# A hybrid attention/SSD decoder layer on one core: last SSD root on VectorE, projection tokens split in pieces, loads further ahead, first quad without hops, conv weights stored later

## The chip, the core and the metric

The kernel runs on one core of one Trainium2 chip. The core has a matrix engine (TensorE, PE in the profile; PEld is its loading of the stationary operand), a vector engine (VectorE, DVE), a scalar engine (ScalarE, ACT), a general engine (GpSimd, POOL) and an engine that issues the DMAs here (SyncE, SP). Each works through its own instructions in order and waits on semaphores for the others. The metric is the device time of one execution in microseconds (us). Before the change three runs gave a median of 2215.1 us (2215.06 to 2215.61).

## The reference

One decoder layer with 2048 tokens and a width of 1024, in float32 (cut to what matters):

```python
h = modulate(rmsnorm(x, norm1_w), shift1, scale1)
proj = h @ w_in
q, k, v, z, xbc, dt_raw = jnp.split(proj, [o1, o2, o3, o4, o5], axis=-1)
q, k = rope(q, positions), rope(k, positions)
attn = sliding_window_attention(q, k, v, sinks)          # window 128
xbc = jax.nn.silu(causal_depthwise_conv(xbc, conv_w, conv_b))
xs, Bm, Cm = jnp.split(xbc, [SSM_WIDTH, SSM_WIDTH + SSM_GROUPS * D_STATE], axis=-1)
y = ssd_chunked_scan(xs, dt, A, Bm, Cm, d_skip) * jax.nn.silu(z)
yg = y.reshape(b, s, SSM_GROUPS, SSM_WIDTH // SSM_GROUPS)
yg = yg * lax.rsqrt(jnp.mean(yg * yg, axis=-1, keepdims=True) + EPS)
x = x + gate1 * (jnp.concatenate([attn, yg * ssm_norm_w], axis=-1) @ w_out)
h = modulate(rmsnorm(x, norm2_w), shift2, scale2)
x = x + gate2 * ((jax.nn.silu(g) * u) @ w_down)          # g, u = split(h @ w_gate_up)
return rmsnorm(x, final_norm_w)
```

The scale, shift and gate vectors come from `silu(c) @ w_ada + b_ada`.

## The kernel before

**Tiling.** The tokens are taken in four blocks (b = 0 to 3) of 512, each of four tiles (t) of 128. Every large product is made of three matmuls: each operand is split into a high part (a copy in a shorter format, made by ACT) and a low part (the remainder, made by DVE), and `mm3` adds high·high, high·low and low·high. A weight is split by `weight`: L274 on ACT and L275 on DVE. Where a weight serves several blocks the split pair is stored to memory (L278) and loaded again by later blocks as one pair (L270, 512 KB) in place of the raw weight (L273, 256 KB).

**Stages.** In the order in which PE runs them: an opening, then for each block the projections `queries`, `keys_values`, `convolved` (the causal convolution, eight channels c, weights `w_x`) and `gated` (z). Between them stand `out_proj(0)` (443 to 509 us), `out_proj(1)` (582 to 635 us) and, from 703.5 us, 22 quads, which compute the gate and up projection of the first half of the tokens. Later come the second half and the down projection.

**Hops.** Attention (`attentions`) and the scan (`ssds`) of a block consist of small steps with few matmuls each. They are woven into the large stages: generators whose steps (`hops`) are taken by `tick(ratio)` after each piece of a large stage, `ratio` being the number of hops for each piece. A pending entry `[n, root]` runs after n ticks. Through the projections PE's order is the order of the program text; the orders of DVE, ACT, POOL and SP are laid by the compiler's scheduler from program order and dependencies, except that `behind(engine)` ties an instruction behind the last one written for that engine.

**What the change touches.** `ssds` ends each tile with a group norm: L813 to L815 form the mean square, `rsqrt` (L246) its root (13 small operations on POOL, L252 to L257, behind L249 and L250 on DVE), `normed` (L734) scales by it on ACT, and the four transposes L739 follow on PE. `mixed` (L827) loads the finished attention and scan outputs of a block (the mix, eight channels) and splits them, L832 on ACT and L833 on DVE; out_proj reads channels 0 to 3 with the first half of a weight and 4 to 7 with the second. `out_proj` loads x (L842), adds the gated product (L849), stores `mid`, and sums the squares (L292); its `root` (L297, four matmuls against ones) gives the reciprocal norm, which `spread` (L333) puts on all partitions. `operands_first`, `operands_between` and `sums_ahead` (L953) make the operands of the quads during out_proj(1), conv(3) and gated(3), and `operands_kept` (L973) splits the last ones within the first quad (L907 on ACT, L908 on DVE or POOL). In the attention, L651 are the score matmuls, L660 their masking on DVE, L669, L670, L673 to L676 and L679 the softmax, L685, L687, L694 and L696 the product with the values. L204 (DVE) belongs to the modulation vectors, L492 and L493 end a channel of the convolution, L510 to L517 are its taps.

Of the kernel before, what the change touches and what calls it, by code (L numbers as in the profile page):

```python
# [32 lines left out]
TMP, M1, M2, M4 = 8, 3, 8, 4  # L33
MIX, MIX2, MIX1, RATIO_UP = 0.78, 1.1, 1.25, 0.7
HALF = 32
# [9 lines left out]
def hymba_layer(ctx, tc, xT, xtok, pos, wada, wadk, vecs, rows, wq, wkv, wz, wx, wo, wgu, wd, outT):  # L45
# [442 lines left out]
    def convolved(b, h):  # L488
# [7 lines left out]
        for c in range(8):  # L496
            ps = dense()
            for half in range(2):
                if half:
                    if ending:  # L500
                        end(*ending.pop())
                    yield
                whi, wlo = weight(wx[c, half], T, ("x", c, half), b == 0)
                for i in range(4):
                    k = 4 * half + i
                    ws = slice(i * P, (i + 1) * P)
                    mm3(ps, whi[:, ws], wlo[:, ws], h[k][0], h[k][1], k == 0, k == KT - 1)
# [190 lines left out]
    def ssds(b, stepping, m):  # L698
# [46 lines left out]
        for t in range(NT):  # L745
# [70 lines left out]
            rs = small([P, 2], "rs", 2)  # L816
            rsqrt(rs, ss, 2, nc.gpsimd, "rss", sb)
            out = (y, o, ts, rs)
# [7 lines left out]

    def mixed(b, mix, cs, into):  # L827
        for c in cs:
            hi, lo = into(c)
            m = lo.bitcast(F32)  # L830
            nc.sync.dma_start(m, spill[b][c])
            nc.scalar.activation(hi, m, AF.Copy)  # L832
            nc.vector.tensor_tensor(lo, m, hi.bitcast(F32), ALU.subtract)  # L833
            mix.append((hi, lo))

    def out_proj(b, y_of, mix, bank_of, acc, norm=None, each=lambda c: None):
        for c in range(KT):
            ps = bank_of(c)
            for half in range(2):
                if half:  # L840
                    x = tmp()
                    nc.sync.dma_start(x, xT[b, c])  # L842
                    yield
                whi, wlo = weight(wo[c, half], T, ("o", c, half), b == 0, b > 1)
                for i in range(4):
                    k = 4 * half + i
                    ws = slice(i * P, (i + 1) * P)
                    mm3(ps, whi[:, ws], wlo[:, ws], mix[k][0], mix[k][1], k == 0, k == KT - 1)
            nc.vector.scalar_tensor_tensor(x, ps, gate1[:, c:c + 1], x, ALU.mult, ALU.add)  # L849
            nc.sync.dma_start(mid[b][c], x)  # L850
            square_into(acc, x, c == 0, nc.vector if b < 2 else nc.gpsimd)
            each(c)
            yield

        def root():
            y_of[b] = rstd(acc, st=norm and norm())
        if norm is None:
            pending.append([2 if b else 9, root])
        else:
            for _ in range(2):  # L860
                yield
            root()
        yield
# [89 lines left out]
    def sums_ahead(s, bc):  # L953

        for k in range(4):
            h = fetched_mid(s, k, ((1, 1),))
            for at, src in (((0, 1), scaled_01[k]), ((0, 0), scaled_d[s][0][k]), ((1, 0), scaled_d[s][1][k])):
                h[at] = fetched_scaled(src)
            yield
            with behind(mybir.EngineType.DVE):  # L960
# [3 lines left out]
            nc.vector.scalar_tensor_tensor(t2, h[0, 0], shift_of(k, 0), t3, ALU.add, ALU.add)  # L964
            nc.vector.scalar_tensor_tensor(t4, h[1, 0], shift_of(k, 1), t2, ALU.add, ALU.subtract)
            if k < 3:
                for to, x in zip(raw_d[k], (h[1, 1], t3, t2, t4)):
                    nc.sync.dma_start(to, x)
            else:
                sums_ahead.last = dict(zip(("b22", "t3", "t2", "t4"), (h[1, 1], t3, t2, t4)))  # L970
            yield

    def operands_kept(ops):  # L973
        for n, src in zip(("t2", "t3", "b22", "t4"), (2, 1, 0, 3)):
# [5 lines left out]
            for k, x in enumerate((*got, sums_ahead.last[n])):  # L980
                if n == "b22":
                    shifted(ops[n][k], x, shift_of(k, 1))
                else:
                    kept(ops[n][k], x, nc.vector if n == "t2" else nc.gpsimd)

# [479 lines left out]
    def beside(main, ratio):  # L1465
        for i, _ in enumerate(main):
            yield i
            tick(ratio)

# [36 lines left out]
    with tc.manual_schedule(engines={mybir.EngineType.PE}):  # L1506
# [35 lines left out]
        for _ in range(4):  # L1542
            tick(MIX2)
        mixed(0, mix, range(KT), lambda c: operand())
        run(g, MIX1)
        run(out_proj(0, y_of, mix, lambda c: dense(), sums()), MIX1)
# [9 lines left out]
        bp = early.enter_context(tc.tile_pool(name="b0", bufs=1, reuse_waits="tile"))  # L1556
        mixed(1, mix, range(KT), lambda c: pair("b", 12, pool=bp))
        ops = {}
        operand_tiles(ops, bp, ("b11",), 12)
        for i in range(6):  # L1560
            take(conv, 1)
            tick(0.5)
            if i == 2:
                dg = diagonal(y_of[0])
            if i == 4:
                bcs = [spread(y_of[0], bc=side_bank(2), dg=dg)]
        prepared(3)
        firsts = operands_first(0, ops, bcs, (0,))
# [6 lines left out]
        for i in beside(chain(conv, gated(3, h)), 0.5):  # L1575
            if i == 3:
                dg = diagonal(y_of[1])
            if i == 5:
                drain(firsts)
                bcs.append(spread(y_of[1], bc=side_bank(3), dg=dg))  # L1580
                firsts = operands_between(0, ops, bcs)
            if i == 10:
                drain(firsts)
                firsts = sums_ahead(0, bcs)
            next(firsts, None)
# [15 lines left out]
    operands_kept(ops)  # L1601
    for _ in beside(main, RATIO_UP):
        if not sides:
            break
# [9 lines left out]
    def loaded(b, c):  # L1614
        mixed(b, mixes[b], (c,), lambda c: pair("mo", 11, pool=op))

# [149 lines left out]
```

## Time and profile before

| | before |
|---|---|
| median of three runs | 2215.1 us |
| profiled execution, its own time | 2213.34 us |
| its span in the trace | 2211.6 us |
| mean granted TensorE clock | 0.989 |
| idle time of PE in the span | 56.1 us |

The profile is of one execution. A timeline row gives start, length, engine, line, operation, output and inputs by the names of the program, shapes, and in brackets the idle time of the engine ahead of it with what ended that time. Times of one row can overlap the next by some hundredths, since the operations of an engine are pipelined. A window row gives the busy time of each engine in a stretch, with the count of instructions, the granted clock of PE (1.00 is full), the share of the DMA engines in use and what they moved.

### The profile page before, as it was taken

The page shows a single profiled execution, that of the slowest core. Times are in us where ns is not written, and L with a number is a line of the kernel's source. Part 1 is how long each engine was busy: PE and PEld are TensorE (multiplying, and loading weights), DVE is VectorE, ACT ScalarE, POOL GpSimd, SP SyncE. Part 2 cuts the span into 40 slices and gives each one's busy share as a digit, 9 for nine tenths or more (in the row PEclk, how much of TensorE's full clock was granted, in tenths as well). Part 3 has the DMA queues.
Part 4 walks back from the last instruction along what each step waited for, and adds up shares of the span by engine and source line. Part 5 has one row for each costly group of instructions (what it writes and reads, how often), then busy time and mean ns, then how long its engine had stood idle before and what let it go on. Part 6 is the DMA issues. An engine that isn't in the chain of part 4 may idle for free.

```text
span 2211.6 us, 33250 instructions
## 1 busy us (share of the span) xinstructions
PE 2155.5 (97%) x10984; PEld 1776.0 (80%) x10984; DVE 1656.8 (75%) x3139; ACT 1010.6 (46%) x2121; POOL 568.3 (26%) x714
## 2 busy tenths in 40 slices
PE   8989998999999999999999999999999999999998
PEld 6879897878778677788888888788888888788887
DVE  6987756776668767688887768878888775786575
ACT  3674634653545555433335445533333334554441
POOL 0213343323102311144442221233322321210011
PEclk9999999999999999999999999999999999999999
DMA  7998888697999422333344687735555536678553
GB/s 271 325 363 303 285 245 278 216 354 231 352 321 330 163 90 86 118 111 112 98 134 154 213 265 263 270 126 177 177 173 186 162 121 218 238 263 275 182 164 103
DMA packets 289756, 470.96 MB, mean 213 GB/s; under 512 B 27440, under 2 KB 97072, under 8 KB 289584
## 3 DMA queue, kind: packets, MB, share of 16 engines
q1 hardware_dynamic: 289008, 468.32, 63.4%
q8 instruction: 86, 1.41, 0.3%
q14 instruction: 86, 0.70, 0.1%
q10 hardware_dynamic: 576, 0.52, 0.1%
HBM read 333.93 MB, written 134.81 MB: 212 GB/s over the span
## 4 chain that ended last, share of the span: by engine, by line
PE 51%; DMA 2%; DVE 2%; POOL 1%; ACT 0%; issue 0%; SPq 0%; DVEq 0%; ACTq 0%; POOLq 0%
PE d L1144 15%; PE d L1014 6%; PE d L1012 6%; PE d L1013 6%; PE d L1285 1%; PE am L1014 1%; PE am L1012 1%; PE am L1013 1%; PE sm L1014 1%; PE sm L1012 1%; PE sm L1013 1%; DMA a<-act_t 1%; PE d L282 1%; PE d L283 1%; PE d L284 1%
## 5 line engine op out<-in xcount | busy, mean ns | idle before, releaser
L1144 PE MATMUL d<-a,w 128*128 128x512 f32 x1716 | 403.6, 396 | 3.6 <-DVE w L1140 2.0
L1144 PEld LDWEIGHTS d<-a,w 128*128 128x128 f32 x1716 | 321.9, 188 | 82.8 <-DVE w L1140 2.9
L1013 PE MATMUL d<-b,w 128*128 128x512 f32 x924 | 366.4, 397 | 0.8 <-POOL b L908 0.8
L1012 PE MATMUL d<-b,w 128*128 128x512 f32 x924 | 365.9, 400 | 0.9 <-ACT t L1044 0.9
L1014 PE MATMUL d<-b,w 128*128 128x512 f32 x924 | 366.0, 398 | 0.0
L873 ACT ACTIVATE w<-s 128x512 fp32r<-128x512 f32 x176 | 110.9, 632 | 219.6 <-PE d L1014 171.9
L1013 PEld LDWEIGHTS d<-b,w 128*128 128x128 f32 x924 | 174.6, 189 | 41.0 <-POOL b L908 1.7
L1012 PEld LDWEIGHTS d<-b,w 128*128 128x128 f32 x924 | 174.2, 189 | 41.1 <-ACT t L1044 1.3
L1014 PEld LDWEIGHTS d<-b,w 128*128 128x128 f32 x924 | 173.8, 188 | 40.0 <-issue 0.4
L282 PE MATMUL d<-w,hl 128*128 128x256 f32 (+1 forms) x592 | 175.2, 296 | 4.2 <-DVE s L515 4.2
L283 PE MATMUL d<-w,hl 128*128 128x256 f32 (+1 forms) x592 | 169.7, 287 | 0.1
L284 PE MATMUL d<-w,hl 128*128 128x256 f32 (+1 forms) x592 | 169.5, 286 | 0.0
L874 DVE TENSOR_TENSOR w<-s,w 128x512 fp32r<-128x512 f32 x176 | 157.8, 898 | 4.3 <-ACT w L873 3.8
L1126 DVE TENSOR_TENSOR a<-a 128x512 fp32r<-128x512 f32 x154 | 108.8, 721 | 50.7 <-ACT a L1125 50.3
L1140 DVE TENSOR_TENSOR w<-raw,w 128x512 fp32r<-128x512 f32 x156 | 111.9, 726 | 38.6 <-ACT w L1139 38.5
L1125 ACT ACTIVATE a<-a 128x512 fp32r<-128x512 f32 x154 | 95.9, 628 | 93.2 <-DMA a<-act_t 57.0
L873 ACT ACTIVATE w<-raw 128x512 fp32r<-128x512 f32 x132 | 83.1, 631 | 118.8 <-PE d L1014 46.2
L292 POOL TENSOR_TENSOR acc<-acc,t 128x512 f32<-128x512 f32 x35 | 52.2, 1492 | 331.4 <-ACT t L291 320.5
L282 PE MATMUL d<-hl,w 128*128 128x512 f32 x320 | 133.7, 418 | 0.7 <-DMA w<-w_x 0.7
L1139 ACT ACTIVATE w<-raw 128x512 fp32r<-128x512 f32 x156 | 90.7, 587 | 81.0 <-PE d L1144 52.3
L284 PE MATMUL d<-hl,w 128*128 128x512 f32 x320 | 127.3, 398 | 0.0
L283 PE MATMUL d<-hl,w 128*128 128x512 f32 x320 | 126.9, 397 | 0.0
(418 smaller groups left out, 4798.5 us busy)
## 6 DMA issues: line engine op xcount, KB each, us to landing
raw<-in_wgu_dram SPq DMA_DIRECT2D x176, 256.0 KB, 2.8
w<-w_x SPq DMA_DIRECT2D x48, 512.0 KB, 6.0
act_t<-t SPq DMA_DIRECT2D x88, 256.0 KB, 3.2
a<-act_t SPq DMA_DIRECT2D x88, 256.0 KB, 4.3
act_b<-t SPq DMA_DIRECT2D x66, 256.0 KB, 2.0
a<-act_b SPq DMA_DIRECT2D x66, 256.0 KB, 4.1
aw<-in_wada_dram SPq DMA_DIRECT2D x64, 256.0 KB, 4.8
raw<-wd_s SPq DMA_DIRECT2D x64, 256.0 KB, 3.0
```

The costliest lines, as they stand in the source:

```text
L282: nc.tensor.matmul(out, ahi, bhi, start=first, stop=False)
L283: nc.tensor.matmul(out, ahi, blo, start=False, stop=False)
L284: mm3.last = nc.tensor.matmul(out, alo, bhi, start=False, stop=last)
L873: nc.scalar.activation(hi, x, AF.Copy)
L874: eng.tensor_tensor(lo, x, hi.bitcast(F32), ALU.subtract)
L1012: nc.tensor.matmul(out, ahi, bhi, start=first and k == 0, stop=False, skip_group_check=True)
L1013: nc.tensor.matmul(out, ahi, blo, start=False, stop=False, skip_group_check=True)
L1014: mm3.last = nc.tensor.matmul(out, alo, bhi, start=False, stop=k == 3, skip_group_check=True)
L1125: nc.scalar.activation(hi, raw, AF.Copy)
L1126: nc.vector.tensor_tensor(lo, raw, hi.bitcast(F32), ALU.subtract)
L1140: nc.vector.tensor_tensor(w[1], raw, w[0].bitcast(F32), ALU.subtract)
L1144: mm3.last = nc.tensor.matmul(ps, w[x][:, ws], act[k][y], start=new and k == 0 and x + y == 0, stop=k == KP - 1 and x == 1, skip_group_che ...
```

## The change

The diff does the following.

1. The split pairs of the convolution's weights are stored when block 1 uses them, not block 0. So conv(1) loads the raw weights and splits them once more, and conv(2) is the first to load the pairs.
2. In `ssds` the root of the last tile of each block runs on DVE (nine operations, L260 to L262) in place of POOL.
3. `mixed` issues its eight loads at once and returns a generator that splits two channels at a time, each tied behind the last instruction written for ACT and for DVE. One pair is split after each piece of gated(2), or of conv(3) ahead of out_proj(1); what is left is split ahead of out_proj. The old form stays in `loaded`, for blocks 2 and 3.
4. `out_proj` loads the x of the next channel one channel ahead (through `load_x`, L345). The root of out_proj(1) runs one tick later, the spreads move by a piece, and `sums_ahead` starts a piece earlier and keeps two loads in flight.
5. In `operands_kept` the remainders of t3 are made by DVE; only those of t4 stay on POOL. The first six pieces of the quads tick with ratio 0, the others with 0.75 (0.7 before).

```diff
@@ constants @@
-MIX, MIX2, MIX1, RATIO_UP = 0.78, 1.1, 1.25, 0.7
+MIX, MIX2, MIX1, RATIO_UP = 0.78, 1.1, 1.25, 0.75
@@ convolved @@
-                whi, wlo = weight(wx[c, half], T, ("x", c, half), b == 0)
+                whi, wlo = weight(wx[c, half], T, ("x", c, half), b == 1)
@@ ssds @@
-            rsqrt(rs, ss, 2, nc.gpsimd, "rss", sb)
+            rsqrt(rs, ss, 2, nc.vector if t == NT - 1 else nc.gpsimd, "rss", sb)
@@ mixed @@
+        got = []
         for c in cs:
             hi, lo = into(c)
-            m = lo.bitcast(F32)
-            nc.sync.dma_start(m, spill[b][c])
-            nc.scalar.activation(hi, m, AF.Copy)
-            nc.vector.tensor_tensor(lo, m, hi.bitcast(F32), ALU.subtract)
-            mix.append((hi, lo))
+            nc.sync.dma_start(lo.bitcast(F32), spill[b][c])
+            got.append((hi, lo))
+
+        def split():
+            for n, (hi, lo) in enumerate(got):
+                with behind(mybir.EngineType.Activation):
+                    nc.scalar.activation(hi, lo.bitcast(F32), AF.Copy)
+                with behind(mybir.EngineType.DVE):
+                    nc.vector.tensor_tensor(lo, lo.bitcast(F32), hi.bitcast(F32), ALU.subtract)
+                mix.append((hi, lo))
+                if n % 2:
+                    yield
+        return split()
@@ out_proj @@
+        nxt = load_x(b, 0)
         for c in range(KT):
-            ps = bank_of(c)
+            ps, x = bank_of(c), nxt
             for half in range(2):
                 if half:
-                    x = tmp()
-                    nc.sync.dma_start(x, xT[b, c])
+                    nxt = load_x(b, c + 1) if c < KT - 1 else None
                     yield
...
-            pending.append([2 if b else 9, root])
+            pending.append([3 if b else 9, root])
@@ sums_ahead @@
+        held = [load(0)]
+        yield
+        held.append(load(1))
+        yield
+        for k in range(4):
+            got = summed(k, held.pop(0))
...
+            yield
+            if k < 2:
+                held.append(load(k + 2))
+                yield
@@ operands_kept @@
-                    kept(ops[n][k], x, nc.vector if n == "t2" else nc.gpsimd)
+                    kept(ops[n][k], x, nc.gpsimd if n == "t4" else nc.vector)
@@ main program @@
-        mixed(0, mix, range(KT), lambda c: operand())
-        run(g, MIX1)
+        split = mixed(0, mix, range(KT), lambda c: operand())
+        for _ in beside(g, MIX1):
+            next(split, None)
+        drain(split)
...
-        mixed(1, mix, range(KT), lambda c: pair("b", 12, pool=bp))
+        split = mixed(1, mix, range(KT), lambda c: pair("b", 12, pool=bp))
...
         for i in range(6):
             take(conv, 1)
             tick(0.5)
-            if i == 2:
+            if i > 1:
+                next(split, None)
+            if i == 1:
                 dg = diagonal(y_of[0])
-            if i == 4:
+            if i == 3:
                 bcs = [spread(y_of[0], bc=side_bank(2), dg=dg)]
+        drain(split)
...
-            if i == 3:
+            if i == 4:
                 dg = diagonal(y_of[1])
...
-            if i == 10:
-                drain(firsts)
-                firsts = sums_ahead(0, bcs)
+            if i == 9:
+                last_of, firsts = firsts, sums_ahead(0, bcs)
+                drain(last_of)
...
-    for _ in beside(main, RATIO_UP):
+    for _ in beside(main, lambda i: RATIO_UP if i >= 6 else 0):
```

In the changed kernel the lines of `mixed` are L837 (ACT, was L832) and L839 (DVE, was L833). Three places show how the orders move.

DVE near the end of gated(2), where a scan step ends (L808, L809), before:

```order
L660 ISA ast 128x1
L833 TENSOR_TENSOR hl_5311<-hl_5311 128x512
L833 TENSOR_TENSOR hl_5315<-hl_5315 128x512
L808 TENSOR_TENSOR m_5019<-m_5019,sm 128x512
L669 TENSOR_SCALAR ast<-ast 128x4
L809 SCALAR_TENSOR_TENSOR m_5019<-m_5019,m_4726 128x512
L670 TENSOR_TENSOR ast<-row,ast 128x4
L833 TENSOR_TENSOR hl_5319<-hl_5319 128x512
```

DVE at the same scan step in the changed kernel (its first two splits are hl_5335 and hl_5337):

```order
L660 ISA ast 128x1
L808 TENSOR_TENSOR m_5063<-m_5063,sm 128x512
L669 TENSOR_SCALAR ast<-ast 128x4
L809 SCALAR_TENSOR_TENSOR m_5063<-m_5063,m_4770 128x512
L670 TENSOR_TENSOR ast<-row,ast 128x4
L754 TENSOR_TENSOR m_5324<-st,dtv 128x512
L755 TENSOR_TENSOR m_5325<-st,row 128x512
L761 TENSOR_TENSOR m_5333<-sm,upper 128x256
L839 TENSOR_TENSOR hl_5335<-hl_5335 128x512
L839 TENSOR_TENSOR hl_5337<-hl_5337 128x512
```

And DVE some 45 rows later in the changed kernel, around the start of out_proj(0), with the splits of channels 4 to 7:

```order
L787 TENSOR_TENSOR m_5659<-st,ex 128x512
L275 TENSOR_TENSOR w<-raw,w 128x512
L728 TENSOR_TENSOR m_5652<-m_5652,m_5333 128x512
L839 TENSOR_TENSOR hl_5343<-hl_5343 128x512
L839 TENSOR_TENSOR hl_5345<-hl_5345 128x512
L527 SCALAR_TENSOR_TENSOR so<-s,d 128x256
L839 TENSOR_TENSOR hl_5347<-hl_5347 128x512
L839 TENSOR_TENSOR hl_5349<-hl_5349 128x512
```

All eight splits move from ahead of L808 to behind it, the last four of them up to the start of out_proj(0).

DVE around the start of out_proj(1) (b is the tile of a split mix channel), before: the last row of one group of maskings, then the last five splits.

```order
L660 ISA ast 128x1
L833 TENSOR_TENSOR b<-b 128x512 x3
L493 SCALAR_TENSOR_TENSOR sx<-s 128x512
L833 TENSOR_TENSOR b<-b 128x512
L669 TENSOR_SCALAR ast<-ast 128x4
L833 TENSOR_TENSOR b<-b 128x512
L204 ISA aw,part<-aw,csil,vec 128x512
```

The same place in the changed kernel, from the last masking of the next group on, with channels 4 and 5 and then 6 and 7:

```order
L839 TENSOR_TENSOR b<-b 128x512 x2
L675 TENSOR_TENSOR ast<-ast 128x4
L493 SCALAR_TENSOR_TENSOR sx<-s 128x512
L669 TENSOR_SCALAR ast<-ast 128x4
L676 RECIPROCAL ast<-ast 128x4
L204 ISA aw,part<-aw,csil,vec 128x512
L204 ISA part 128x1
L670 TENSOR_TENSOR ast<-row,ast 128x4
L204 ISA aw,mod<-aw,csil,part 128x512
L204 ISA mod 128x1
L1468 TENSOR_TENSOR dsh<-mod 128x4
L839 TENSOR_TENSOR b<-b 128x512 x2
```

The last four splits move behind one more group of four maskings (L660) and the last two behind L675 and what follows it.

ACT at the end of the third tile of ssds(1) (t = 2), during queries(3), at 514 us, before:

```order
L734 ACTIVATE m_6059<-m_6059,rs 128x256 x2
L687 COPY m_6406<-am 128x4x128
L687 COPY m_6406<-at 128x4x128
L673 ACTIVATE m_6340,ast<-m_6340,ast 128x256 x2
L673 ACTIVATE m_6343,ast<-m_6343,ast 128x256 x2
L742 ACTIVATE m_6219<-st,vec 128x128 x4
```

The same in the changed kernel:

```order
L687 COPY m_6450<-am 128x4x128
L673 ACTIVATE m_6384,ast<-m_6384,ast 128x256 x2
L673 ACTIVATE m_6387,ast<-m_6387,ast 128x256 x2
L687 COPY m_6450<-at 128x4x128
L674 ACTIVATE ast<-ast 128x4
L734 ACTIVATE m_6105<-m_6105,rs 128x256 x2
L679 ACTIVATE m_6384<-m_6384,ast 128x256 x2
L679 ACTIVATE m_6387<-m_6387,ast 128x256 x2
L742 ACTIVATE m_6265<-st,vec 128x128 x4
```

L734 moves from ahead of an attention step's L687 and L673 to behind them.

More of the change, by code (lines that the diff above doesn't have):

```diff
@@ L953, in sums_ahead, with load @@
     def sums_ahead(s, bc):
-        for k in range(4):
+        def load(k):
             h = fetched_mid(s, k, ((1, 1),))
@@ L958, in sums_ahead, with summed @@
                 h[at] = fetched_scaled(src)
-            yield
+            return h
+        def summed(k, h):
             with behind(mybir.EngineType.DVE):
@@ L965, in sums_ahead @@
             nc.vector.scalar_tensor_tensor(t4, h[1, 0], shift_of(k, 1), t2, ALU.add, ALU.subtract)
+            return h[1, 1], t3, t2, t4
+        held = [load(0)]
[4 more added lines that the diff above has]
+            got = summed(k, held.pop(0))
             if k < 3:
-                for to, x in zip(raw_d[k], (h[1, 1], t3, t2, t4)):
+                for to, x in zip(raw_d[k], got):
                     nc.sync.dma_start(to, x)
             else:
-                sums_ahead.last = dict(zip(("b22", "t3", "t2", "t4"), (h[1, 1], t3, t2, t4)))
+                sums_ahead.last = dict(zip(("b22", "t3", "t2", "t4"), got))
             yield
+            if k < 2:
+                held.append(load(k + 2))
+                yield
     def operands_kept(ops):
@@ L1467, in beside @@
             yield i
-            tick(ratio)
+            tick(ratio(i) if callable(ratio) else ratio)
     def run(main, ratio):
@@ L1614, in loaded @@
     def loaded(b, c):
-        mixed(b, mixes[b], (c,), lambda c: pair("mo", 11, pool=op))
+        hi, lo = pair("mo", 11, pool=op)
+        m = lo.bitcast(F32)
+        nc.sync.dma_start(m, spill[b][c])
+        nc.scalar.activation(hi, m, AF.Copy)
+        nc.vector.tensor_tensor(lo, m, hi.bitcast(F32), ALU.subtract)
+        mixes[b].append((hi, lo))
     def first_output():
```

## The prediction

> **What bounds the kernel now.** I read the shares of busy time first, then the PE rows that begin after idle time, then windows laid around those rows.
>
> ```profile
> span 2211.6 us, 33250 instructions
> PE 2155.5 (97%) x10984; PEld 1776.0 (80%) x10984; DVE 1656.8 (75%) x3139; ACT 1010.6 (46%) x2121; POOL 568.3 (26%) x714
> ```
>
> TensorE has matmuls in flight for 2155.5 of 2211.6 us, and the change gives it neither fewer nor other matmuls. So only the 56.1 us in which it idles, and the time in which its clock is low, can be won. The PE timeline names what each idle stretch waited for (start, length, engine, line, and in brackets the idle time before the row):
>
> ```profile
> 129.89 0.58 PE L282 MATMUL d<-w,hl 128*128 128x256 f32 x1 [4.20 <-DVE s L515]
> 146.47 0.82 PE L616 MATMUL at<-ident,m 128*128 128x128 f32 x3 [2.14 <-DMA m<-q]
> 154.67 0.38 PE L651 MATMUL at<-k_ring,m 64*128 64x256 f32 x1 [2.87 <-DVE m L620]
> 367.96 0.90 PE L739 MATMUL st<-ident,m 128*128 128x128 f32 x3 [6.75 <-ACT m L734]
> 423.65 0.80 PE L759 MATMUL sm<-m 128*128 128x128 f32 x2 [3.52 <-DVE m L808]
> 514.61 0.44 PE L739 MATMUL st<-ident,m 128*128 128x128 f32 x2 [1.46 <-ACT m L734]
> 642.13 1.01 PE L297 MATMUL d<-ones,acc 128*128 128x2 f32 x4 [3.67 <-DVE acc L292]
> 709.91 1.43 PE L651 MATMUL am<-k_ring,m 64*128 64x256 f32 x5 [1.52 <-ACT m L696]
> 726.48 0.50 PE L1013 MATMUL d<-b,w 128*128 128x512 f32 x1 [0.52 <-POOL b L908]
> 730.73 0.51 PE L1013 MATMUL d<-b,w 128*128 128x512 f32 x1 [0.26 <-POOL b L908]
> ```
>
> These ten are the gaps in the part that is rewritten; together 26.9 us. A gap costs more than its length. In the windows behind six of them (columns: busy time of PE, PEld, DVE, ACT, POOL, then the granted clock, the DMA share and GB/s) PE works at half clock:
>
> ```profile
> 129.90:133.00 3.10, 3.10 (x15) 3.10 (x16) 1.18 (x1) 2.44 (x7) 1.22 (x2) 0.52 1.05 390
> 368.00:371.60 3.60, 3.60 (x11) 2.91 (x12) 0.03 (x1) 1.45 (x5) 0.00 (x0) 0.50 0.70 209
> 423.60:430.00 6.40, 6.35 (x30) 6.13 (x32) 4.29 (x12) 3.49 (x14) 1.24 (x2) 0.51 0.12 40
> 515.00:518.40 3.40, 3.40 (x18) 3.39 (x18) 0.45 (x2) 3.40 (x13) 0.00 (x0) 0.53 0.63 224
> 642.00:648.20 6.20, 6.07 (x18) 5.18 (x19) 4.34 (x21) 0.00 (x0) 0.00 (x0) 0.50 1.02 326
> 710.00:716.30 6.30, 6.30 (x20) 5.35 (x21) 6.30 (x16) 2.18 (x6) 1.51 (x1) 0.50 0.97 337
> 70.00:130.00 60.00, 55.67 (x275) 45.92 (x273) 56.84 (x137) 40.39 (x68) 19.37 (x27) 1.00 1.02 372
> 200.00:260.00 60.00, 59.33 (x302) 46.97 (x301) 45.21 (x108) 39.51 (x97) 22.28 (x42) 1.00 0.88 300
> ```
>
> At half clock half of the busy time is lost: about 1.5, 1.8, 3.1, 1.6, 3.0 and 3.1 us. The 1.46 us gap at 514.61 already has such a window behind it. The Trainium skill ("TensorE: Matmul & The Clock Gate", Part 1) has idle gaps above about 3 us as what brings the clock down; the 514.61 row with its 0.53 behind it speaks against that, so a new stall of 2 to 3 us is charged here with its slow stretch, and by the page's rule the sum below would be about 3.5 us lower.
>
> **The change part by part.** All sums are in the profiled execution's own 2213.34 us (span 2211.6 and 1.7 around it); the median of the runs, 2215.1, lies 1.8 above it, and 1.8 is added at the end. Minus is a gain.
>
> *w_x stored in conv(1), 70–160 and 200–260.* Sixteen stores of 512 KB leave conv(0), where the DMA share is 1.02. But the window 70:130 also has DVE busy for 56.84 of 60 us, and the gap at 129.89 waits for a DVE operation. The splits that stand ahead of it (L275) all stay, so relief of the DMA alone can return at most the 3.2 us in which DVE idles. The 2.14 us wait for q: its load is now issued on SP behind two loads of xs (L702), which wait for the last xs stores, so I keep it and let it grow by 1.4. The 2.87 us wait for L620 I let go, since that row comes earlier in DVE's order. Sum −1.5; bounds −10.7 (all three gaps and 1.5 of clock) and +4. In conv(1) sixteen splits come back:
>
> ```profile
> L275 DVE TENSOR_TENSOR w<-raw,w x92: 673/688/1797, 60.2 to 1311.6; 128x512 fp32r<-128x512 f32 x80, 128x528 fp32r<-128x528 f32 x12
> L274 ACT ACTIVATE w<-raw x92: 612/632/651, 58.5 to 1309.6; 128x512 fp32r<-128x512 f32 x80, 128x528 fp32r<-128x528 f32 x12
> ```
>
> 16 × 0.69 = 11.0 us more on DVE (45.21 to 56 of 60) and 16 × 0.63 = 10.1 on ACT (39.5 to 50). Loads of 16 × 256 KB and stores of 16 × 512 KB replace loads of 16 × 512 KB: 4.2 MB more, 300 to 370 GB/s, where 390 GB/s stand in the row of 129.90. It fits, but barely, and the probabilities of an attention block queue behind splits on DVE. I take +2; bounds 0 and +5 (as full as 70:130, which lost 4.3 us of PE).
>
> *Last root of a block on VectorE.* ssds(0) ends its root here (POOL and DVE timelines, then ACT):
>
> ```profile
> 355.14 3.00 DVE L833 TENSOR_TENSOR hl<-hl 128x512 fp32r<-128x512 f32 x3
> 358.06 0.67 DVE L808 TENSOR_TENSOR m<-m,sm 128x512 f32<-128x512 f32 x1
> 361.32 0.17 DVE L250 TENSOR_SCALAR rs<-rss 128x2 int32<-128x2 int32 x1
> 362.24 0.75 DVE L515 SCALAR_TENSOR_TENSOR s<-d,vec,s 128x512 f32<-128x512 f32 x1 [0.74 <-ACT s L513]
> 361.18 0.19 POOL L252 TENSOR_SCALAR rss<-ss 128x2 f32<-128x2 f32 x1 [3.59 <-DVE ss L815]
> 362.96 0.74 POOL L255 TENSOR_TENSOR rss<-rss 128x2 f32<-128x2 f32 x1
> 367.17 0.20 POOL L257 TENSOR_TENSOR rs<-rss,rs 128x2 f32<-128x2 f32 x1
> 367.40 0.91 ACT L734 ACTIVATE m<-m,rs 128x256 f32<-128x256 f32 x2
> ```
>
> Thirteen POOL operations take from 361.18 to 367.37, 6.2 us. On DVE they are nine of 0.17, some 1.8 us with issue, but DVE's new order puts L515, L516 and both L204 between them (4 × 0.7 = 2.8, by the L515 row), and on ACT the convolution's L492 stands ahead of L734. So the root itself wins little over 1 us; the three L833 of 3.00 us, which leave the place ahead of L808, let the chain begin up to 2.4 us earlier, part of which the convolution takes back. I take −2.6 of the 6.75, with the slow stretch kept; bounds −8.5 (gap and slow stretch gone) and 0. The Trainium skill ("SBUF — State Buffer", on two separate sides) says that a GpSimd instruction and a VectorE one with two SBUF inputs lock each other out of a shared port; the L255 row of 0.74, beside L515 and among siblings of 0.20, agrees, and would put the root's gain at the three stretched operations, about 1.4 us, near what is taken.
>
> *Splits of the mix in pairs, gated(2).* The gap at 423.65:
>
> ```profile
> 420.45 0.69 DVE L833 TENSOR_TENSOR hl<-hl 128x512 fp32r<-128x512 f32 x1 [1.53 <-ACT hl L832]
> 422.31 0.69 DVE L833 TENSOR_TENSOR hl<-hl 128x512 fp32r<-128x512 f32 x1 [1.17 <-ACT hl L832]
> 422.92 0.68 DVE L808 TENSOR_TENSOR m<-m,sm 128x512 f32<-128x512 f32 x1
> ```
>
> DVE waits 1.53 and 1.17 us for mix rows with L808 queued behind. In the new order L808 follows the L660 rows directly: 3.52 and 3.1 us of slow clock go, −6.6. What is late next is the second half of out_proj(0)'s first output: its splits for channels 4 and 5 now stand behind L787 and L728, which wait for matmuls just ahead of it on PE. L726 on ACT, L728, a weight split and the split itself follow one another, four of 0.7 (by the L808 row): 2.9 us with the handovers, an estimate, and 1.5 of clock. Sum −2.2; bounds −6.6 and +2.
>
> *ssds(1).* ACT's row shows L734 now behind four L673 and L674, which wait for L669; four L673 take 2.0 us by the row of 593.89 below. The root is sooner by as much as at 361 at best. +2 (gap 1.46 to 3.5); bounds −3 (gap and slow stretch gone) and +4.
>
> *Splits for out_proj(1).* Rows of DVE and ACT around its start:
>
> ```profile
> 585.30 0.68 DVE L833 TENSOR_TENSOR b<-b 128x512 fp32r<-128x512 f32 x1
> 588.64 0.47 DVE L660 CUSTOM_DVE_ANT_0 m<-am,amask,row 128x256 f32<-128x256 f32 x1
> 595.59 0.16 DVE L675 TENSOR_TENSOR ast<-ast 128x4 f32<-128x4 f32 x1 [2.32 <-ACT ast L674]
> 593.89 0.49 ACT L673 ACTIVATE m<-m,ast 128x256 f32<-128x256 f32 x1
> 586.01 0.28 PE L651 MATMUL am<-k_ring,m 64*128 64x256 f32 x1
> ```
>
> Now the last split ends at 585.98, and PE goes from L651 (586.2) straight into channels 4 to 7. After, channels 4 and 5 stand behind four L660 that need those L651: 4 × 0.47 and the split's 0.7 from 586.0 on put channel 4 at 588.6, some 2.3 us after PE wants it. Channels 6 and 7 stand behind L675, L493, two L204 and more, that is behind a whole softmax on ACT: another 3.0. With 2.0 of clock, +7.3. Bounds 0 (if DVE catches up) and +12 (if they end where the next softmax has its L675 now, 595.59, with the first half's 2.6 us of other work ahead of them).
>
> *Root of out_proj(1) one step later.* L297 moves behind twelve matmuls. By the window 200:260 (302 in 59.33 us) one takes 0.2, and these, 512 wide, a little more: 2.7 us, which leave 1.0 of the 3.67; a gap so short I take to bring no slow stretch, and its 3.0 go too: −5.7; bounds −6.7 and 0. *x and sums loaded ahead*: no row above waits for them; nothing, covered by PE's matmuls; at worst the x load lies behind an output's store on SP, which the bounds of the last part cover.
>
> *First quad.* The t3 splits leave POOL:
>
> ```profile
> L908 POOL TENSOR_TENSOR b<-t,b x20: 1281/1297/8159, 677.2 to 1398.3; 128x512 fp32r<-128x512 f32 x20
> L908 DVE TENSOR_TENSOR b<-t,b x12: 675/684/1783, 719.4 to 1398.8; 128x512 fp32r<-128x512 f32 x12
> ```
>
> Four of 1.30 become four of 0.68 on DVE, and the 0.52 and 0.26 go. The hops that "without hops" should take away stand in PE's order within the first quad as before, moved by a dozen matmuls, so 1.52 with 3.1 of clock are not counted as won. −1.5; bounds −7.5 and +3.
>
> Sum: −1.5 + 2 − 2.6 − 2.2 + 2 + 7.3 − 5.7 − 1.5 = −2.2, or 2211.1 by the profile and **2212.9 us** as a median.
>
> **Rivals.** *A, the gaps go and nothing takes their place*: the splits catch up. Then 7.3 + 4.4 + 2 leave the sum: −15.9, or about 2199 (2190 with conv(0)'s gaps as well). For it: DVE is busy only 75% of the span. Against it: DVE runs in order, and the splits are tied behind rows that wait for PE. *B, slower*: the splits for out_proj(1) come at their upper bound, +12 and 3.1 us for two slow stretches instead of 7.3, and conv(1) costs 5: −2.2 + 7.8 + 3 = +8.6, about 2224. It decides when channels 6 and 7 are ready later than some 590 us, that is when L675 ahead of them waits for its softmax. *C, the slots merely swap*: what goes at 423 and 642 comes back at 447 and 586, total −1 to +3, about 2216; that is the forecast's upper part. *D, the change does not do what it says*: true of "without hops" by the order of PE; for the rest the order shows the moves, so only the first quad's term hangs on it: about 2214.
>
> **How the numbers follow.** The forecast's own case (2207 to 2218) has 0.48, A 0.27, B 0.15, C beyond that and D 0.10. The range leaves out A's far end and B's: 2197 to 2222. A measurement here can tell 0.2%, 4.4 us, from no change. Faster than 2210.7: A and a third of the forecast's case, 0.43; slower than 2219.5: most of B and a little of C, 0.18; between them 0.39.
>
> **What would show it.** Right: no gap at L297 of out_proj(1) nor at L759 in gated(2); new PE gaps released by DVE b of the splits at out_proj(1)'s first output, and by DVE hl at out_proj(0)'s; a gap of about 4 us at the last L739 of ssds(0); POOL no longer a releaser of L1013. Wrong: out_proj(1) starting without a gap (then A), the 129.89 gap gone (then DVE was not its bound), or PE waits of several us within 200 to 260 (then conv(1) was underpriced).

## The result and the profile after

| | before | changed |
|---|---|---|
| median of five runs | 2215.1 us | 2224.13 us |
| lowest to highest | 2214.06 to 2215.61 | 2222.07 to 2228.12 |
| ratio | | 1.0043, 95% interval 1.0028 to 1.0057 |
| profiled execution | 2213.34 us | 2224.71 us |
| its span | 2211.6 us | 2223.0 us |

The changed kernel is slower by 0.4%: 11.4 us in the profiled spans. The page of the changed kernel, its first lines:

```profile
span 2223.0 us, 33256 instructions
PE 2154.6 (97%) x10984; PEld 1775.6 (80%) x10984; DVE 1660.7 (75%) x3195; ACT 1017.4 (46%) x2135; POOL 549.9 (25%) x658
```

PE has the same 10984 matmuls in flight for 2154.6 us, 0.9 us less than before, and idles for 68.4 us where it idled for 56.1. So the loss is in waits again, and the PE timeline of the changed kernel names them (start, length, engine, line, and in brackets the idle time ahead of the row):

```profile
131.00 0.58 PE L282 MATMUL d<-w,hl 128*128 128x256 f32 x1 [6.65 <-DVE s L515]
150.60 1.09 PE L616 MATMUL at<-ident,m 128*128 128x128 f32 x4 [3.26 <-DMA m<-q]
366.58 1.12 PE L739 MATMUL st<-ident,m 128*128 128x128 f32 x4 [4.55 <-ACT m L734]
433.20 0.84 PE L739 MATMUL st<-ident,m 128*128 128x128 f32 x4 [2.02 <-ACT m L734]
444.44 0.50 PE L282 MATMUL d<-hl,w 128*128 128x512 f32 x1 [2.63 <-ACT hl L837]
445.94 0.51 PE L283 MATMUL d<-hl,w 128*128 128x512 f32 x1 [1.00 <-DVE hl L839]
517.64 1.04 PE L739 MATMUL st<-ident,m 128*128 128x128 f32 x4 [4.14 <-ACT m L734]
587.36 0.50 PE L283 MATMUL d<-b,w 128*128 128x512 f32 x1 [0.41 <-DVE b L839]
597.58 0.80 PE L282 MATMUL d<-b,w 128*128 128x512 f32 x1 [6.51 <-ACT b L837]
726.74 0.49 PE L1034 MATMUL d<-b,w 128*128 128x512 f32 x1 [2.13 <-ACT b L916]
1217.63 0.79 PE L282 MATMUL am<-mo,w 128*128 128x512 f32 x1 [5.80 <-ACT mo L1645]
```

The gaps at L759 (3.52), at L297 (3.67) and at L1013 (now L1035) released by POOL are gone. The largest of what came is at out_proj(1), 6.51, and one that no term of the prediction speaks of, at the first matmul of out_proj(2), 5.80.

Since PE runs the same matmuls in nearly the same order, the place of each loss can be read by comparing the start of the n-th matmul in both traces. How far the changed kernel lies behind, and what that changed by, in us:

| up to matmul | place (time before) | behind before | change |
|---|---|---|---|
| 400 | opening and kv(0) (76) | −0.4 | −0.4 |
| 1200 | conv(0), gated(0), queries(1), kv(1) (210) | 0.8 | +1.2 |
| 2000 | conv(1), gated(1) (325) | 0.8 | 0.0 |
| 2400 | last root of ssds(0) (406) | −1.0 | −1.8 |
| 2600 | end of gated(2) (436) | −7.5 | −6.5 |
| 2800 | start of out_proj(0) (470) | 0.1 | +7.6 |
| 3200 | ssds(1), third tile (535) | 3.0 | +2.9 |
| 3400 | keys_values(3) (560) | 4.1 | +1.0 |
| 3600 | start of out_proj(1) (599) | 14.2 | +10.1 |
| 4000 | root of out_proj(1) (682) | 7.3 | −6.9 |
| 4400 | first quad (755) | 8.0 | +0.7 |
| 6400 | hops beside the quads (1171) | 4.8 | −3.3 |
| 6800 | start of out_proj(2) (1260) | 12.1 | +7.3 |
| end | the rest | 11.4 | −0.7 |

How far two profiles can be compared in this way differs from place to place. Over all the runs below, those with the same edits agree to some 0.1 us at the end of gated(2) and at the root of out_proj(1). In the first 210 us they do not: the kernel before and four of the runs below (all with the store in conv(0)) have the same instructions in the same order on DVE, ACT, POOL and SP up to 276 us, and yet lie up to 2.2 us apart at matmul 400 and up to 3.9 us at matmul 1200. A part of that is the clock: a gap of 2.87 us at 154.67 of the kernel before has full clock behind it, the gap of 2.96 us at the same matmul of a kernel with the same order (the run of x ahead alone) half clock (windows of the two):

```profile
154.60:158.00 3.40, 3.33 (x31) 3.20 (x32) 3.40 (x12) 0.00 (x0) 0.00 (x0) 1.00 1.00 325
152.60:156.00 3.40, 3.36 (x19) 3.14 (x20) 3.40 (x11) 0.00 (x0) 0.00 (x0) 0.50 0.98 287
```

Total times scatter too: the unchanged kernel took 2208.85 to 2224.2 us in the 27 runs beside one group of kernels below.

At out_proj(1) the timelines of PE, DVE and ACT show what PE waited for:

```profile
586.56 0.39 PE L282 MATMUL d<-b,w 128*128 128x512 f32 x1
589.76 0.40 PE L284 MATMUL d<-b,w 128*128 128x512 f32 x1
592.73 1.29 DVE L839 TENSOR_TENSOR b<-b 128x512 fp32r<-128x512 f32 x2
593.94 0.16 DVE L675 TENSOR_TENSOR ast<-ast 128x4 f32<-128x4 f32 x1
597.56 1.29 DVE L839 TENSOR_TENSOR b<-b 128x512 fp32r<-128x512 f32 x2 [1.07 <-ACT b L837]
595.32 1.69 ACT L679 ACTIVATE m<-m,ast 128x256 f32<-128x256 f32 x4
596.91 1.13 ACT L837 ACTIVATE b<-b 128x512 fp32r<-128x512 f32 x2
```

The twelve matmuls from 586.56 to 589.76 are those of channels 0 to 3, so the 0.41 us at 587.36 is a wait for the low part of channel 0. In the kernel's text channel 4 comes next, and PE has wanted it since 591.07. The pair that DVE splits at 592.73 is done by 594.02 and does not release PE; the last pair does, as soon as its first copy (L837 at 596.91) ends. So the pair at 592.73 is channels 6 and 7, and channels 4 and 5 come last, not the other way round as the order ahead of the prediction was read. Their copies stand on ACT behind the four L679 of a softmax, and DVE (L839) waits for them. At out_proj(2) a chain crosses every engine (timelines of PE, ACT and SP of the changed kernel):

```profile
1210.53 0.60 PE L739 MATMUL st<-ident,m 128*128 128x128 f32 x4
1211.16 1.14 ACT L742 ACTIVATE m<-st,vec 128x128 f32<-128x128 f32 x4 [1.82 <-PE st L739]
1212.33 0.38 SPq L743 DMA_DIRECT2D mix<-m  x1
1213.99 5.88 SPq L1644 DMA_DIRECT2D mo<-mix  x11
1216.95 0.63 ACT L1645 ACTIVATE mo<-mo 128x512 fp32r<-128x512 f32 x1 [4.12 <-DMA mo<-mix]
```

The last transposes of the last scan, their scaling, the store of the mix, the load of it, the copy: 7.1 us from L739 to the first matmul that needs it. In the order of PE the first matmul of out_proj(2) stood 46 rows behind the last transposes before, and stands 4 behind them now, so PE stands in front of the chain. Windows behind the two waits, and conv(1)'s (busy PE, PEld, DVE, ACT, POOL, clock, DMA share, GB/s):

```profile
597.50:604.00 6.50, 6.42 (x16) 4.79 (x17) 2.23 (x5) 3.82 (x13) 0.00 (x0) 0.54 0.00 0
1217.60:1221.40 3.80, 3.77 (x9) 2.56 (x10) 2.49 (x4) 2.39 (x4) 0.00 (x0) 0.52 1.02 346
200.00:260.00 60.00, 60.00 (x312) 48.02 (x311) 50.91 (x117) 44.46 (x108) 23.57 (x40) 1.00 0.98 345
```

Half clock adds about 3 us to the 6.51 and 1.8 to the 5.80. Conv(1), with the sixteen splits and the stores, has no PE idle time at all.

### The profile page after: what moved, and what is told of

It reads as the page before. It is cut to its first block, busy times and chain, and to the rows that moved or that the text cites. A ratio compares the mean times of both kernels' runs of the same rounds, so it can differ in the third digit from the quotient of the medians.

```text
span 2223.0 us, 33256 instructions
## 1 busy us (share of the span) xinstructions
PE 2154.6 (97%) x10984; PEld 1775.6 (80%) x10984; DVE 1660.7 (75%) x3195; ACT 1017.4 (46%) x2135; POOL 549.9 (25%) x658
## 4 chain that ended last, share of the span: by engine, by line
PE 88%; DVE 4%; DMA 4%; ACT 2%; issue 1%; POOL 0%; SPq 0%; DVEq 0%; ACTq 0%; POOLq 0%
PE d L1166 15%; PE d L1034 10%; PE d L1036 10%; PE d L1035 10%; PE d L282 7%; PE d L283 7%; PE d L284 7%; PE d L1307 1%; PE am L1036 1%; PE am L1034 1%; PE am L1035 1%; PE am L694 1%; PE sm L806 1%; DMA a<-act_t 1%; PE sm L1036 1%
## 5 line engine op out<-in xcount | busy, mean ns | idle before, releaser
L1035 PE MATMUL d<-b,w 128*128 128x512 f32 x924 | 367.3, 397 | 0.3 <-DVE b L917 0.2
L1035 PEld LDWEIGHTS d<-b,w 128*128 128x128 f32 x924 | 174.8, 189 | 41.0 <-DVE b L917 1.1
L1161 ACT ACTIVATE w<-raw 128x512 fp32r<-128x512 f32 x156 | 90.9, 588 | 87.6 <-PE d L1166 56.1
```

The lines of the kernel that those rows point to most:

```text
L1035: nc.tensor.matmul(out, ahi, blo, start=False, stop=False, skip_group_check=True)
```

## The experiments

Each kernel below was timed in three rounds beside the kernel before; ratios are to it. First, parts of the change undone one at a time.

**The store of the conv weights back in conv(0).**

```diff
-                whi, wlo = weight(wx[c, half], T, ("x", c, half), b == 1)
+                whi, wlo = weight(wx[c, half], T, ("x", c, half), b == 0)
```

> The changed kernel (2224.1 us) with the conv weights stored in conv(0) again, the rest as changed. Theory: between 100 and 210 us the later store lost 1.25 us against before (PE runs 0.44 us ahead at the 400th matmul and 0.81 behind at the 1200th), because the bank of conv(0)'s last channel waits for VectorE and not for a DMA; that comes back here. A second effect comes with it: in this kernel's order 35 PE rows instead of 4 lie between the last transposes of ssds(3) and out_proj(2)'s first matmul, so the 5.8 us gap at 1217.6 should be under 1 us. Together about 8 us less, 2214 to 2218. Rival: the relief of the DMAs is a gain that other waits hide; then this kernel is 2 us or more slower than the changed one in the 100 to 260 us part, and if the gap at 1217.6 comes from late transfers it stays.

2219.06 us (1.0016, 1.0006 to 1.0026). The gap at out_proj(2) went, and the stretch around it took 7.3 us less. But up to matmul 1200 this kernel is 2.1 us slower than the changed one, not 1.25 faster: the theory's first half is not borne out. Two waits of the attention's first tiles and one for a weight pair stand here (PE timeline of this kernel):

```profile
151.04 0.39 PE L651 MATMUL am<-k_ring,m 64*128 64x256 f32 x1 [3.04 <-ACT m L619]
154.39 0.58 PE L651 MATMUL at<-k_ring,m 64*128 64x256 f32 x1 [2.96 <-DVE m L620]
207.50 0.50 PE L282 MATMUL d<-hl,w 128*128 128x512 f32 x1 [1.72 <-DMA w<-w_x]
```

The later store also changed VectorE's order: the gap of 6.65 us at 131.00 in the changed kernel is 4.22 here and 4.20 before. Whether it is a gain in all, this pair can't say, for this kernel lies 2.9 us behind the kernel before at matmul 1200 with the same order up to there.

**The splits for out_proj(1) at once.** The old loop is called for block 1 in place of the generator.

```diff
-        split = mixed(1, mix, range(KT), lambda c: pair("b", 12, pool=bp))
+        mixed_now(1, mix, range(KT), lambda c: pair("b", 12, pool=bp))
+        split = iter(())
```

> The changed kernel with the eight splits for out_proj(1) written at once as before (they still end ahead of the second group of maskings), the rest as changed. Theory: the 6.5 us gap at 597.6 and the 0.4 at 587.4 go, with some 3 us of half clock behind them: 9 to 10 us less, 2213 to 2216, and the last L837/L839 pair ends before PE asks for channel 4. Rival: VectorE is simply full there (11.27 of 13 us in 582 to 595 before), so the wait moves to another place of out_proj(1), and the time stays within 3 us of 2224.

2215.4 us (1.0002, 0.9992 to 1.0011). At the start of out_proj(1) 10.1 us come back and stay. PE goes into channel 4 (the thirteenth matmul of out_proj(1)) without a wait, and DVE's last three splits begin at 587.62, ahead of the second group of maskings at 591.49 (PE and DVE timelines of this kernel):

```profile
589.29 0.50 PE L282 MATMUL d<-b,w 128*128 128x512 f32 x1
587.62 1.89 DVE L833 TENSOR_TENSOR b<-b 128x512 fp32r<-128x512 f32 x3
591.49 0.48 DVE L660 CUSTOM_DVE_ANT_0 m<-am,amask,row 128x256 f32<-128x256 f32 x1
```

**Out_proj(2) two steps later.**

```diff
+        for _ in range(2):
+            yield
         for c in range(KT):
             loaded(2, c)
```

> The changed kernel with two empty steps at the head of first_output, so that out_proj(2)'s first matmul stands 40 PE rows behind the last transposes of ssds(3) (4 in the changed kernel, 46 before). Theory: the chain transposes, L742, store, load, split takes 7 us (1210.5 to 1217.6) and 40 rows of quads (some 9 us) cover it; the 5.8 us gap at 1217.6 and its half clock go: 6 to 8 us less, 2216 to 2218. Rival: the gap comes from the last hop itself being late, through its root on VectorE; then PE meets the wait wherever out_proj(2) stands and at least 3 us of it stay.

2215.88 us (1.0000, 0.999 to 1.001): 8.2 us under the changed kernel, 7.4 of them at that place. The last transposes run at 1214.65 and the first matmul of out_proj(2) 9.5 us later without a wait (PE timeline of this kernel):

```profile
1214.65 0.60 PE L739 MATMUL st<-ident,m 128*128 128x128 f32 x4
1224.18 0.39 PE L282 MATMUL am<-mo,w 128*128 128x512 f32 x1
```

**The splits for out_proj(0) at once.**

```diff
-        split = mixed(0, mix, range(KT), lambda c: operand())
-        for _ in beside(g, MIX1):
-            next(split, None)
-        drain(split)
+        mixed_now(0, mix, range(KT), lambda c: operand())
+        run(g, MIX1)
```

> The changed kernel with the eight splits for out_proj(0) written at once as before, the rest as changed. Theory: the spread splits gave 6.5 us at the end of gated(2) and took back 7.6 up to the middle of out_proj(0) (2.0 at 433.2, 2.6 at 444.4, 1.0 at 445.9 and half clock), so undoing them changes the total by no more than 2 us: 2222 to 2226, with the 3.5 us gap at L759 back and those three gone. Rival, the prediction's own term (a net gain of 2.2): 2226 or more.

2222.09 us (1.0027, 1.0014 to 1.004), 2.0 under the changed kernel. The old gap at L759 is back with 3.08 us, the waits at 433.2, 444.4 and 445.9 are gone, which gives 2.8 us; the gap at the last L739 of ssds(0) grows from 4.55 to 6.11 and takes 1.4 back. The pieces bring no gain at out_proj(0).

**One part alone: the root of out_proj(1) one tick later, in the kernel before.**

```diff
-            pending.append([2 if b else 9, root])
+            pending.append([3 if b else 9, root])
```

> The kernel before with one part of the change alone: the root of out_proj(1) one tick later (3 for 2, and the diagonal that reads it one piece later). Theory: L297 stands twelve matmuls later, the 3.67 us gap at 642 and the 6.8 us of half clock behind it (3.4 us lost) go, as they did in the changed kernel, and nothing takes their place: 6 to 7 us under the kernel before, 2208 to 2210. Rival: in the changed kernel the gap went because out_proj(1) itself had been held up for 6.5 us at its start, which gave the sums time; then alone at least 2 us of the gap stay and the time is within 3 us of before.

2218.0 us (1.0002, 0.9988 to 1.0017): the theory fell. L297 stands later and still waits as long (PE timeline of this kernel, then the DVE row of the kernel before that the expectation of a later run rests on):

```profile
644.53 1.82 PE L297 MATMUL d<-ones,acc 128*128 128x2 f32 x8 [3.57 <-DVE acc L292]
639.94 0.75 DVE L849 SCALAR_TENSOR_TENSOR t<-d,mod,t 128x512 f32<-128x512 f32 x1 [2.92 <-DMA t<-in_xT_dram]
```

The second row is what the prediction overlooked: the last sum waits for its x from memory. The rival's numbers came, but not its cause: with the splits at once (the second run) out_proj(1) is not held up, and L297 has no gap. The first quad of this kernel came out 7.0 us longer in another order and the hops after it 3.2 us shorter, which is the rest of the difference in the total.

**Out_proj(2) later, and every last root on GpSimd again.**

> The changed kernel with out_proj(2) two steps later (2215.9 us as measured) and, beside that, the last root of every scan on GpSimd again. Theory: of the gap at the last transposes of ssds(0), 6.75 us before and 4.55 now, the root on VectorE gave only some 0.6 (with it and the old splits the gap was 6.11), so this one is 5.0 to 5.5 us and the time 2215 to 2218. Rival: the root gave all of it; then the gap is 6.5 us or more and the time 2218 or more.

2218.61 us (1.0006, 0.9993 to 1.002). The gap of the last root is 5.25 us against 4.54 with the root on VectorE, so the engine of the root is worth 0.7 us there, beside the splits in pieces. Beside the old splits it shows no gain: the gap is 6.11, 7.61, 8.01 and 7.14 us in the four runs with the splits for out_proj(0) at once and the root on VectorE, and 6.75, 7.26 and 6.89 in the kernel before and the two with one part of the change alone. The rest of the total lies elsewhere: 2.8 us less between matmuls 3200 and 3600, nearly all in keys_values(3), 3.5 more in the first quad and 2.5 more in the hops beside the quads.

**Two causes out, and three.** Splits for out_proj(1) at once with out_proj(2) later; then the splits for out_proj(0) at once too.

> The changed kernel with two causes taken away together: the splits for out_proj(1) at once as before, and out_proj(2) two steps later. Theory: the two waits are independent, 10.0 and 7.4 us by the kernels with one of them undone, so 2224.1 less 17.4, 2205 to 2209, under both kernels. Rival: one covers the other (what is won at 598 us lets the quads meet a later wait); then 2211 or more.

> As the kernel before this one, and the splits for out_proj(0) at once too. Theory: by the kernel with this alone undone it is worth another 1.4 to 2 us: 2203 to 2208. Rival: the pieces at out_proj(0) are a gain of about 2 us once the rest is right; then 2209 or more.

2210.01 us (0.9969, 0.9957 to 0.9981), and 2206.29 us (0.9951, 0.9933 to 0.9968). The two waits add up: 9.9 and 7.7 us at their places. The total missed the expected 17.4: the median is 14.1 under the changed kernel's and the profile 11.6 shorter. Up to matmul 3200 that profile had lost 4.3 us at places no edit of it touches. The third part gave 3.7 in the times, more than the 2.0 it gave alone; both are near what such comparisons scatter by.

**x ahead in out_proj(1) alone, in the kernel before.** `out_proj` gets `ahead = b == 1`: with it x is loaded a channel ahead, without it as before.

> The kernel before with one part of the change alone: x loaded one channel ahead, and only in out_proj(1). Theory: the gap at L297 (3.67 us before, 3.57 with the root one tick later) is the wait of L849 for its x (2.92 us in the row of 639.94), so the gap and its half clock go, 5 to 7 us at that place, with the root where it was. The first quad's order may add or take some 3 us of its own. Rival: both edits are needed, or the wait is for the sums themselves; then a gap of 2 us or more stays at L297.

2209.35 us (0.9970, 0.9955 to 0.9985). The gap at L297 is gone with the root where it was, 6.8 us at that place (PE timeline of this kernel):

```profile
640.53 0.95 PE L297 MATMUL d<-ones,acc 128*128 128x2 f32 x8
```

**x as before in the changed kernel, out_proj(2) later.**

> The changed kernel with out_proj(2) two steps later (2215.9 us) and x loaded as before, beside its use. Theory: the 3.7 us gap at L297 of out_proj(1) comes back with half clock, 5 to 7 us, though the root still runs one tick later; 2218 to 2223, since the gap at ssds(1)'s third tile (4.36 us) may shrink by up to 3 with VectorE's order. Rival: the root's tick holds the gap off; then L297 shows less than 1 us and the time is under 2218.

2213.47 us (0.999, 0.9979 to 1.0001): the rival was right. The last sum does wait for its x (the DVE row of L858), but L297 meets no gap (652.04, PE row):

```profile
648.73 0.75 DVE L858 SCALAR_TENSOR_TENSOR t<-d,mod,t 128x512 f32<-128x512 f32 x1 [5.30 <-DMA t<-in_xT_dram]
652.04 0.95 PE L297 MATMUL d<-ones,acc 128*128 128x2 f32 x8
```

So x ahead removes the wait for x, and the later root can cover it here by twelve matmuls. In the kernel before, the later root alone did not. Two things differ there: the squares (L291) stood behind three operations of a convolution tap on ACT, so that the sum ran 3.5 us after its x, here 1.5; and the load of x was issued 0.4 us behind the transposes L616 (635.17 and 634.80), here 2.6 us ahead of them (643.46 and 646.04), so that x itself was earlier for PE. Which of the two decides is not shown.

**x ahead only in out_proj(1), in the fastest version.**

> The fastest so far (both groups of splits at once, out_proj(2) two steps later; 2206.3 us) with x loaded ahead in out_proj(1) alone. Theory: the gap at the third tile of ssds(1) (4.27 us) comes from L250 standing behind the four maskings L660 on VectorE, and that order came with the earlier x loads of out_proj(0); here L249 and L250 stand ahead of them as in the kernel before, so the gap is 1.5 us again: 2202 to 2206. Rival: it comes from another edit; then 3.5 us or more stay.

**2203.19 us (0.9943, 0.9924 to 0.9962)**, the fastest of all. The gap at ssds(1)'s third tile is 1.46 us as in the kernel before (PE row of this kernel), and the order of DVE explains it: L250 at 505.62, ahead of the maskings from 507.12 on, where the changed kernel has them from 509.76 and L250 only at 512.83. There ACT had done with L674 by 516.23 and then waited for the root (last three rows: DVE and ACT of the changed kernel).

```profile
511.04 0.84 PE L739 MATMUL st<-ident,m 128*128 128x128 f32 x4 [1.46 <-ACT m L734]
505.62 0.16 DVE L250 TENSOR_SCALAR rs<-rss 128x2 int32<-128x2 int32 x1
507.12 0.47 DVE L660 CUSTOM_DVE_ANT_0 m<-am,amask,row 128x256 f32<-128x256 f32 x1
509.76 0.47 DVE L660 CUSTOM_DVE_ANT_0 m<-am,amask,row 128x256 f32<-128x256 f32 x1
512.83 0.15 DVE L250 TENSOR_SCALAR rs<-rss 128x2 int32<-128x2 int32 x1
517.08 0.91 ACT L734 ACTIVATE m<-m,rs 128x256 f32<-128x256 f32 x2 [0.85 <-POOL rs L257]
```

That the x loads of out_proj(0) alone bring the other order is not shown: with x as before throughout but the splits in pieces, the kernel above still had L250 behind the maskings and a gap of 4.16.

**The store back in conv(0), in the fastest version but one.**

> The fastest so far (2206.3 us) with the conv weights stored in conv(0) again. Theory, from the kernel with this alone undone: up to the 1200th matmul the later store is worth 2 us, so this one is slower there by 2 and takes 2207 to 2210. Rival, the first reading of the changed kernel against the one before: the later store costs 1.3 us there; then 2203 to 2206.

2210.63 us (0.9978, 0.9965 to 0.999), 4.3 over the version it starts from; between matmul 400 and 1200 it falls behind by 3.9. With the first run above that would make the later store a gain of 2 to 4 us, but profiles with the same order scatter by more in this stretch: against the kernel before, the four runs with the store in conv(0) fall behind by 0.1 to 5.8 us between those marks, the nine kernels with the later store by −0.7 to 2.1. The size of the gain, and whether there is one, stay open.

## Why the prediction was wrong

The time came out 11 us above the forecast and 2 above the range; the sign of rival B was right, its mechanism half of the cause. Two steps failed most. Nothing behind the first quad had a term, and out_proj(2) lost 7.3 us there; and the splits, taken at +5.1 in sum for out_proj(0) and out_proj(1), came to +11.2. By the steps:

- *Splits for out_proj(1)*: taken at +7.3 with bounds 0 and +12, measured +10.1. That splits would stand behind a whole softmax on ACT and DVE was right; which ones was not. The prediction put channels 4 and 5 at 588.6 (2.3 us late) and channels 6 and 7 another 3.0 later. Channels 6 and 7 were split by 594.0, and channel 4, which PE takes before them, came last: one wait of 6.51 us in place of two. The rival's point of decision, channels 6 and 7 later than 590 us, was passed.
- *What no term held*: out_proj(2), +7.3. The prediction looked for waits where the text of the program changed, and has no term for the hops beside the later quads. The change as a whole moved the end of the last scan next to its consumer: the order of PE has 4 rows in place of 46. Which edit moved it isn't settled: with the store undone alone there are 35 rows again, and with either group of splits undone alone still 4; the roots and the x loads were undone only beside the later out_proj(2), and the ratio of hops never.
- *Splits in gated(2)*: −6.6 and +4.4 were taken, −6.5 and +7.6 came. The first half was exact. Of the second, 2.63 + 1.00 with its slow stretch was foreseen as 2.9 and 1.5; the 2.02 us wait for L734 was not: its root on GpSimd ended only at 432.15, and L837 and L339 held it on ACT to 432.64.
- *Root of out_proj(1)*: −5.7 taken, −6.9 measured, for the wrong reason, so the number was luck: alone the later root gained nothing, and x ahead alone gained 6.8. "No row above waits for them", the prediction said of the x loads; a row of DVE did, 2.92 us at 639.94. It looked at what PE waited for and not one step further.
- *Last root on VectorE*: −2.6 taken, −1.8 came, of which the root itself gives 0.7 by its gap. (The prediction has the stretched L255 row of 362.96 beside L515; it lies beside L516, which starts at 362.90 as L515 ends.)
- *ssds(1)'s third tile*: +2 taken, +2.9 measured, by another order than the one that was read: not L673 and L674 ahead of L734 on ACT, but the four maskings ahead of L250 on DVE, which made the root late.
- *conv(1)*: +2 taken, 0.0 measured; DVE reached 50.91 us of 60 and the DMAs 345 GB/s, less than 56 and 370 by the sum of the parts, and nothing on PE waited. *conv(0)*: −1.5 taken, +1.2 measured for everything in that stretch, which is less than profiles of one order differ by there.
- *First quad*: −1.5 taken, +0.7 measured. The 0.52 and 0.26 for POOL went, but PE now waits 2.13 us for a copy on ACT (L916, at 726.74). The hops beside the later quads gave 3.3 that were not counted.

The places with a term sum to 1.2 + 0.0 − 1.8 − 6.5 + 7.6 + 2.9 + 10.1 − 6.9 + 0.7 = +7.3, where −2.2 was forecast; those without one add −0.4 + 1.0 − 3.3 + 7.3 − 0.7 = +3.9. The prediction charged gaps of 2 to 3 us with a slow stretch, against the rule of the Trainium skill ("TensorE: Matmul & The Clock Gate", Part 1) that idle gaps above about 3 us bring the clock down. The traces are divided. The window behind the gaps of 2.63 and 1.00 us at 444 is slow (first row, the same columns), the one behind the gap of 2.02 us at 433.20 is not (second row). And the gap of 1.46 us at ssds(1)'s third tile has 0.53 behind it in the kernel before, but full clock in the fastest kernel (third row). So a short gap can bring half clock, and its length alone does not tell whether it will.

```profile
444.40:448.20 3.80, 2.75 (x7) 1.99 (x8) 3.80 (x7) 1.82 (x4) 0.34 (x1) 0.77 0.96 313
433.20:436.60 3.40, 3.40 (x28) 3.20 (x29) 3.40 (x9) 3.40 (x10) 0.00 (x0) 1.00 0.75 203
511.00:514.40 3.40, 3.36 (x27) 3.16 (x28) 0.89 (x6) 3.40 (x12) 0.00 (x0) 1.00 0.77 263
```

## What to carry to other kernels

Work that is cut into pieces and tied behind what an in-order engine happens to do inherits the waits of all that work. Pieces that are each tied behind whatever was written last need not run in their own order either, as channels 6 and 7 ahead of 4 and 5 show; ask for each piece when its consumer comes. Where a consumer in a fixed order follows a chain over several engines, count the rows of other work between the chain's head and the consumer, and do it everywhere the order changed, not only where the text did. When an engine waits for a sum, follow the sum's own inputs one step further before deciding which edit will help.

## What the runs showed of the hardware

An x load of 256 KB took a median of 5.3 us to land at out_proj(1) (610 to 645 us of the kernel before), among the 512 KB loads of weight pairs, and 3.5 us at out_proj(2) (1190 to 1278 us). VectorE waited for x at both, 8.4 us in six waits and 2.4 in three, but PE stood behind such a wait only at out_proj(1). The whole time of the unchanged kernel scattered by 0.7% in one group of runs, more than the 0.2% that the prediction took as what a measurement can tell.
